# Attention 0 of a two-layer encoder: three kinds of small transfers issued from GpSimd's queue instead of SyncE's

## The chip, the cores and the metric

The kernel runs on one NeuronCore of a Trainium2 chip. The core has five engines with a queue of instructions each: TensorE (PE, with its weight loads shown as PEld), VectorE (DVE), ScalarE (ACT), GpSimd (POOL) and SyncE (SP), which here does nothing but issue DMAs. Engines wait for each other and for DMAs through semaphores, and a waiting instruction holds all that stands behind it in its queue. The metric is device time in microseconds of one execution, lower is better; times compared are medians of several runs.

## The reference

Two layers work on 1024 tokens of width 1024 in f32. Layer 0, which the change is about, is differential attention with 8 heads. Each head has two query/key pairs of width 64 (c = 0, 1) and values of width 128:

```
sc = einsum('bqhcd,bkhcd->bhcqk', qb, k) * scale
p  = softmax(sc); p = p[:, :, 0] - lam * p[:, :, 1]
o  = einsum('bhqk,bkhd->bqhd', p, v)
o  = rmsnorm(o, subln_g) * (1 - lambda_init)
y  = (o.reshape(b, s, 1024) * silu(z)) @ w_out
```

q, k, v and z are one projection of the normalised input; q and k are turned by a rotary embedding. Layer 1 is latent attention with 8 heads, whose queries have a part without and a part with rotary embedding. Each layer ends in an output projection, a gate and a residual, and a last norm closes the trunk.

## The kernel before, in words

Every f32 operand of a matmul is split into a high part (a cast to fp32r) and a low part (the difference), and a product is three matmuls: high by high, low by high, high by low. In layer 0 the queries of a head have only 64 rows for each c, so high and low keys are stacked in one tile of 128 rows, and the query parts are stored twice. `stack_q` (L361 to L370) makes these tiles for one head and one half of the tokens (512): ScalarE casts the high part `qa` (L364, L365), GpSimd subtracts the low part `qb` (L366, L367), each into one group of 64 partitions, and four DMAs of 128 KB copy them to the other 64 partitions (L369, L370, for `qa` and then for `qb`). The scores (L866) of c = 0 need the first copy of each, those of c = 1 the second. Layer 1 uses the same helper for its rotary query parts (tiles `qpa`, `qpb`).

Attention 0 is a loop over 8 heads of 8 tiles of 128 queries. A tile (`q_tile`) computes scores, two softmaxes and their difference; between its pieces TensorE takes steps of `stream0`, the projections of the next head's k, q and z strips, which are what `rope` and `stack_q` then work on. So a head's query tiles come into being while the head before is computed. `rope` copies the projection to SBUF on ScalarE (L331, L333), swaps rows with four DMAs (L335), and multiplies and adds on GpSimd (L336, L341, L343); the strips' own splits are ScalarE's casts and GpSimd's subtractions (L218, L219).

The tail of a tile (transposes L395, their evictions L397 on ScalarE and L398 on VectorE, the product with v) runs one or two tiles later, in `after_scores`. After a half of a head the output `o` is evicted (L931, L932), multiplied by the gate on GpSimd (L938), and the sum of squares gives the norm: VectorE's few small steps, GpSimd's power (L169) and a small multiplication (L953) yield the factors `y`, 128x4. `finish` applies them. The factors must lie along the free dimension of all partitions, so `bcast_rows` writes them to DRAM (L420, 2 KB) and loads them back spread over all partitions (L422, 256 KB, tile `bc_s`); GpSimd multiplies (L908, `scale`) and a DMA stores the result (L912, `store`, 256 KB). The last half of head 7 goes another way, without these transfers.

The list `hooks` spaces these steps out: what is in it when `after_scores` begins is run at that tile's end, and what a hook appends comes a tile later. Before the change `bcast_rows` is called with the norm, `scale` one tile later (two for the last two halves that take this way), `store` two tiles after `scale`.

A planner orders each engine's instructions from its own estimates. Instructions wrapped in `in_turn` keep the program's order on their engine; nearly all GpSimd work of the attention stages is wrapped. DMAs of SP mostly are not, so the planner may issue them earlier or later than they are written. During attention 0 GpSimd also prepares combinations of the output weights (L1112 to L1123) and of finished outputs (L1145 to L1149), and near its end the splits of the output projection's operands (L1199). SP issues everything: the strips' weights (L197), the rope swaps, the copies, the factors, the stores, the output weights.

Of the kernel before, what the change touches and what calls it, by code (L numbers as in the profile page):

```python
# [11 lines left out]
F32 = mybir.dt.float32  # L12
# [9 lines left out]
P = 128  # L22
# [4 lines left out]
HF = 512  # L27
NH = 8
# [48 lines left out]
def f32v(ap):  # L77
    return ap.bitcast(F32)
# [3 lines left out]
def trunk(ctx: ExitStack, tc: tile.TileContext, A, out):  # L82
    nc = tc.nc
    SP, PE, V, S, G = nc.sync, nc.tensor, nc.vector, nc.scalar, nc.gpsimd

    def pool(stack, name, bufs=1, side="left", space=None):
        kw = dict(name=name, bufs=bufs, reuse_waits="tile")
        if space is not None:
            kw["space"] = space
            if space == DRAM:  # L90
                kw.pop("reuse_waits")
        else:
            kw["side"] = side
        return stack.enter_context(tc.tile_pool(**kw))
# [21 lines left out]
    def bank(tag, name, shape=None):  # L116
        nonlocal turn
        if tag == "acc":
            turn += 1
            if (turn - 1) % (2 + NB.get("accx", 0)) < 2:  # L120
                return psa.tile([P, HF], F32, name=name, tag="acc", bufs=2)
            tag = "accx"
        return ps.tile(shape or [P, HF], F32, name=name, tag=tag, bufs=NB[tag])

    dr = pool(ctx, "dr", bufs=1, space=DRAM)
# [6 lines left out]
    oF = [dr.tile([NH, 2, P, HF], F32, name=f"oF{l}") for l in range(2)]  # L132
# [47 lines left out]
    def behind(eng):  # L180

        return tc.issue_after(mk[eng]) if eng in mk else nullcontext()

    def in_turn(ins):

        return tc.keep_in_program_order(ins) if mk else ins
# [174 lines left out]
    def stack_q(qa, qb, r):  # L361

        with behind("S"):
            S.copy(qa[0:64, 0, :], r[0:64])  # L364
            S.copy(qa[64:128, 1, :], r[64:128])  # L365
        in_turn(G.tensor_sub(qb[0:64, 0, :], r[0:64], f32v(qa[0:64, 0, :])))  # L366
        in_turn(G.tensor_sub(qb[64:128, 1, :], r[64:128], f32v(qa[64:128, 1, :])))  # L367
        for t in (qa, qb):
            SP.dma_start(f32v(t[64:128, 0, :]), f32v(t[0:64, 0, :]))  # L369
            SP.dma_start(f32v(t[0:64, 1, :]), f32v(t[64:128, 1, :]))  # L370

    def store_v(l, sp, acc, tt, fh, tag="vst", bufs=None):
        v = sp.tile([P, 2, HF], F32R, name="v_hl", tag=tag, bufs=bufs or VB[l])
# [43 lines left out]
    def bcast_rows(sp, y, tag, bufs):  # L417

        d_ = dr.tile([HF], F32, name="bc_d", tag="bcd", bufs=4)
        SP.dma_start(d_.rearrange("(p t) -> p t", p=P), y)  # L420
        b = sp.tile([P, HF], F32, name="bc_s", tag=tag, bufs=bufs)
        SP.dma_start(b, d_[None, :].to_broadcast([P, HF]))  # L422
        return b, b.rearrange("p (q t) -> p t q", t=4)

    def t3(ap_):
        return ap_.rearrange("p (t q) -> p t q", t=4)
# [173 lines left out]
    for f in range(2):  # L600
        fs = slice(f * HF, f * HF + HF)
        spread = PE.matmul(cb[:, fs], ones[0:1, :], crow[0:1, fs], start=True, stop=True).ins
# [179 lines left out]
    def q_done(h):  # L782
        def f(acc, half):
            rot, fin = rope(wp, acc, half, SC0, *[G if h else V] * 2)

            def g():
                qa = a0a.tile([P, 2, HF], F32R, name="qa", tag="qs", bufs=4)
                qb = a0a.tile([P, 2, HF], F32R, name="qb", tag="qs", bufs=4)
                stack_q(qa, qb, r.pop() if r else fin())
                QS.setdefault(h, [None, None])[half] = qa, qb  # L790

            r = []
            sum_ = [lambda: r.append(fin()), None] if 0 < h < 5 else []
            side.add(*[None] * ROT, rot, *[None] * (DEF - 1 - ROT - (h == NH - 1)), *sum_, g)
        return f
# [105 lines left out]

    def finish(o, y, l, h, half, dst, ap_, dgs):

        if dst is None:
            b, rb = bcast_rows(ap_, y, "osq", 4)

            def scale():
                in_turn(G.tensor_mul(t3(o), t3(o), rb))  # L908
                hooks.append(lambda: hooks.append(store))

            def store():
                SP.dma_start(oF[l][h, half], o)  # L912

            if l == 0 and (h, half) >= (NH - 2, 1):
                hooks.append(lambda: hooks.append(scale))
            else:
                hooks.append(scale)
            return
        rb = bank("z", "rb") if l else Y[1]
        for j in range(4):  # L920
            js = slice(j * P, (j + 1) * P)
            S.mul(dgs[:, js], ident, y[:, j : j + 1])
            PE.matmul(rb[:, js], ones, dgs[:, js], start=True, stop=True)
        V.tensor_mul(o, o, rb)
# [9 lines left out]
    def subln(o, sq, zz, half, h, dst):  # L934


        if dst is None:
            in_turn(G.tensor_mul(o, o, GZ[h][half]))  # L938
        else:
            V.tensor_mul(o, o, GZ[h][half])  # L940

        def rest():
            pt = Y[0] if dst is not None else ssq_at[0] if ssq_at else bank("acc", "ssq")
            for j in range(4):
                PE.matmul(pt[:, j : j + 1], sq[:, j * P : (j + 1) * P], ones[:, 0:1], start=True, stop=True)
            w = sm.tile([P, 4], F32, name="sl_w")
            fin = sm.tile([P, 4], F32, name="sl_f")
            V.tensor_mul(fin, zz, zz)
            V.scalar_tensor_tensor(out=w, in0=fin, scalar=P * EPS / GUARD ** 2, in1=pt[:, 0:4], op0=ALU.mult, op1=ALU.add)
            V.scalar_tensor_tensor(out=fin, in0=fin, scalar=FMAX / GUARD ** 2, in1=w, op0=ALU.mult, op1=ALU.is_ge)  # L950
            V.tensor_scalar(w, w, 3.0e38, None, op0=ALU.min)
            y = rsqrt(w, 4)
            in_turn(G.tensor_mul(y, y, fin))  # L953
            if dst is not None:
                return lambda: finish(o, y, 0, h, half, dst, None, sq)
            finish(o, y, 0, h, half, None, a0b, sq)

        if dst is None:
            (hooks if h < NH - 1 else rests).append(rest)
        else:  # L960
            return rest()
# [29 lines left out]
    tails, hooks = [None, None], []  # L991
# [171 lines left out]
    class Seven:  # L1163
# [32 lines left out]
        def put(self, raw, hi, lo, eng):  # L1196
            with behind("S"):
                S.copy(hi, raw)  # L1198
            sub = eng.tensor_sub(lo, raw, f32v(hi))  # L1199
            if eng is G:  # L1200
                in_turn(sub)
                self.sub = sub.ins
# [818 lines left out]
    def qp_done(h):  # L2021
        def f(acc, half):
            rot, fin = rope(wp, acc, half, SC1, G, G if h or half else V)

            def g():
                qa = ap.tile([P, 2, HF], F32R, name="qpa", tag="qps", bufs=4)
                qb = ap.tile([P, 2, HF], F32R, name="qpb", tag="qps", bufs=4)
                stack_q(qa, qb, fin())
                QP.setdefault(h, [None, None])[half] = qa, qb

            side.add(None, rot, *[None] * (h > 0 and not half))
            if h and half:
                late_q.append(g)
            elif half:
                first_q.append(g)
            else:
                side.add(g)
        return f
# [35 lines left out]
    def attn1(h, fills, extra=None, late=None):  # L2074
# [5 lines left out]
        def close(half, o_, zz):  # L2080
            if late and half == 1:
                ctx_["late"] = late(o_, zz, ctx_["gz"])
                return
            o = ap2.tile([P, HF], F32, name="o1", tag="o", bufs=2)
            V.scalar_tensor_tensor(out=o, in0=o_, scalar=0.5, in1=ctx_["gz"], op0=ALU.mult, op1=ALU.mult)
            V.reciprocal(zz, zz)
            finish(o, zz, 1, h, half, None, ap2, None)
# [365 lines left out]
```

## Time and profile before

| | us |
|---|---|
| median of 3 runs | 1396.26 (1395.49 to 1396.42) |
| the profiled execution | 1394.95 |
| its span, first to last instruction | 1393.2 |
| TensorE busy | 1367.5 |
| VectorE busy | 928.3 |
| GpSimd busy | 753.1 |
| ScalarE busy | 740.9 |

The granted TensorE clock is 0.999 of full speed. All 230.74 MB of the program's own DMA traffic runs on SP's queue, 52.7% of the time of the 16 DMA engines. Attention 0 lies between 137 us (its first scores) and about 690 us.

How to read it: a row of a group gives line, engine, operation, the tiles written and read, the count, then the busy time and the mean of one, and after the second bar the idle time of the engine before them and what ended it. A row of waits gives total, times and the longest. A row of the timeline gives start and length in us and, in brackets, the idle time before it. SP's issues are sequencer work (SPq) and not counted as busy. TensorE's matmuls overlap and their ends are modelled, so small gaps do not show.

### The profile page before, as it was taken

How to read it: one execution, taken by the hardware profiler on the slowest of the kernel's cores; microseconds unless marked ns; L12 is line 12 of the kernel's file. 1: busy time of each engine (PE TensorE's matmuls, PEld its weight loads, DVE VectorE, ACT ScalarE, POOL GpSimd, SP SyncE). 2: the span in 40 equal slices, each digit the busy share in tenths (PEclk: the TensorE clock that was granted, in tenths of full speed). 3: DMA queues.
4: the chain of work that ended last, by engine and by line, in shares of the span. 5: the costliest groups of instructions: out<-in, count | busy, mean ns of one | idle time of the engine just before them, and what ended most of it. 6: DMA issues, size and time to landing. Idle time of an engine off the chain costs nothing.

```text
span 1393.2 us, 20695 instructions
## 1 busy us (share of the span) xinstructions
PE 1367.5 (98%) x7334; PEld 1144.7 (82%) x7334; DVE 928.3 (67%) x1313; ACT 740.9 (53%) x1339; POOL 753.1 (54%) x593
## 2 busy tenths in 40 slices
PE   9999999999999999999999999999999999999997
PEld 6788888888888887887887888888888888888886
DVE  7655777777666666668596976545656555555684
ACT  5532465656565555567648553335454544545554
POOL 5424374758686858575794233532141373834673
PEclk9999999999999999999999999999999999999999
DMA  9857644343444434526564246489443364667463
GB/s 342 263 177 244 201 110 141 100 144 105 149 127 144 128 121 122 151 61 212 182 219 167 68 137 212 137 282 286 125 105 119 102 201 136 193 221 215 145 245 121
DMA packets 149386, 232.06 MB, mean 167 GB/s; under 512 B 20641, under 2 KB 57633, under 8 KB 149282
## 3 DMA queue, kind: packets, MB, share of 16 engines
q1 hardware_dynamic: 149282, 230.74, 52.7%
q8 instruction: 58, 0.95, 0.3%
q14 instruction: 46, 0.38, 0.1%
HBM read 144.74 MB, written 61.81 MB: 148 GB/s over the span
## 4 chain that ended last, share of the span: by engine, by line
PE 79%; DVE 6%; DMA 5%; ACT 3%; POOL 3%; issue 2%; SPq 1%; POOLq 0%; ACTq 0%; DVEq 0%
PE s L2067 10%; PE acc L173 9%; PE acc L175 9%; PE acc L174 9%; PE tr L395 7%; PE s L866 7%; PE pv L173 4%; PE pv L174 4%; PE pv L175 4%; PE vps L173 2%; PE vps L174 1%; PE vps L175 1%; PE zacc L175 1%; PE zacc L173 1%; PE zacc L174 1%
## 5 line engine op out<-in xcount | busy, mean ns | idle before, releaser
L397 ACT CAST pth<-tr 128x512 fp32r<-128x512 f32 x256 | 150.3, 587 | 285.7 <-PE tr L395 280.8
L412 DVE TENSOR_REDUCE nm<-s 128x1 f32<-128x1024 f32 x192 | 233.8, 1218 | 79.8 <-PE s L866 70.9
L398 DVE TENSOR_TENSOR ptl<-tr,pth 128x512 fp32r<-128x512 f32 x256 | 176.1, 688 | 150.3 <-ACT pth L397 146.3
L219 POOL TENSOR_TENSOR wl<-wraw,wh 128x512 fp32r<-128x512 f32 (+2 forms) x77 | 98.8, 1284 | 208.4 <-ACT wh L218 176.3
L414 ACT ACTIVATE e<-s,nm 128x1024 f32<-128x1024 f32 x128 | 143.5, 1121 | 35.4 <-DVE nm L412 35.0
L395 PE MATMUL tr<-ident,e 128*128 128x128 f32 x1024 | 155.0, 273 | 4.1 <-DVE ptl L398 3.8
L395 PEld LDWEIGHTS tr<-ident,e 128*128 128x128 f32 x1024 | 120.7, 140 | 46.5 <-DVE ptl L398 24.1
L173 PE MATMUL acc<-h0h,wh 128*128 128x512 f32 x360 | 150.2, 417 | 0.0
L173 PE MATMUL pv<-pth,vt 128*128 128x256 f32 x512 | 147.5, 288 | 0.0
L174 PE MATMUL pv<-ptl,vt 128*128 128x256 f32 x512 | 145.6, 284 | 0.0
L175 PE MATMUL pv<-pth,vt 128*128 128x256 f32 x512 | 144.6, 282 | 0.0
L175 PE MATMUL acc<-h0h,wl 128*128 128x512 f32 x360 | 141.5, 393 | 0.0
L174 PE MATMUL acc<-h0l,wh 128*128 128x512 f32 x360 | 141.1, 392 | 0.0
L336 POOL TENSOR_TENSOR rp_r<-rp_raw,cosT 128x512 f32<-128x512 f32 x36 | 47.0, 1305 | 104.4 <-ACT rp_raw L333 52.9
L173 PEld LDWEIGHTS pv<-pth,vt 128*128 128x128 f32 x512 | 97.2, 190 | 2.9 <-ACT pth L397 0.2
L174 PEld LDWEIGHTS pv<-ptl,vt 128*128 128x128 f32 x512 | 97.4, 190 | 2.4
L175 PEld LDWEIGHTS pv<-pth,vt 128*128 128x128 f32 x512 | 97.3, 190 | 0.0
L1199 POOL TENSOR_TENSOR wol<-wol,woh 128x512 fp32r<-128x512 f32 x56 | 82.3, 1492 | 26.0 <-ACT woh L1198 24.4
L866 PE MATMUL s<-ks,qa 128*128 128x512 f32 x256 | 82.7, 403 | 4.4 <-DVE e L874 3.2
L874 DVE SCALAR_TENSOR_TENSOR e<-s,z,e 128x1024 f32<-128x1024 f32 x64 | 82.2, 1284 | 2.2
L866 PE MATMUL s<-ks,qb 128*128 128x512 f32 x256 | 79.8, 393 | 1.2 <-DMA qb<-qb 1.2
L175 PEld LDWEIGHTS acc<-h0h,wl 128*128 128x128 f32 x360 | 67.6, 188 | 15.1
(427 smaller groups left out, 3461.1 us busy)
## 6 DMA issues: line engine op xcount, KB each, us to landing
ada<-in_ada_ss SPq DMA_DIRECT2D x32, 512.0 KB, 5.9
wraw<-in_w_s SPq DMA_DIRECT2D x64, 256.0 KB, 2.8
vS<-v_hl SPq DMA_DIRECT2D x32, 512.0 KB, 5.9
vt<-vS SPq DMA_DIRECT2D x32, 512.0 KB, 4.9
wol<-tS SPq DMA_DIRECT2D x56, 256.0 KB, 5.2
tS<-ob SPq DMA_DIRECT2D x48, 256.0 KB, 2.0
rp_sw<-rp_raw SPq DMA_DIRECT2D x160, 64.0 KB, 2.0
bc_s<-bc_d SPq DMA_DIRECT2D x34, 256.0 KB, 4.2
```

The costliest lines, as they stand in the source:

```text
L173: PE.matmul(psum, ah, bh, start=first, stop=False, skip_group_check=skip)
L174: PE.matmul(psum, ah, bl, start=False, stop=False, skip_group_check=skip)
L175: mm3.last = PE.matmul(psum, al, bh, start=False, stop=last, skip_group_check=skip).ins
L219: sub = (V if pair_of else G).tensor_sub(l_[:, :n], raw[:, :n], f32v(h_[:, :n]))
L395: transpose_p.last = PE.transpose(tr[:, j, :], p[:, kt * P : (kt + 1) * P], ident).ins
L397: mk["S"] = S.copy(pth[kh][:, :, dst], tr).ins
L398: mk["V"] = V.tensor_sub(ptl[kh][:, :, dst], tr, f32v(pth[kh][:, :, dst])).ins
L412: mk["V"] = V.reduce_max(nm, s_ps, axis=AX.X, negate=True).ins
L414: mk["S"] = S.activation(e, s_ps, AF.Exp, bias=nm, scale=1.0, accum_out=zs).ins
L866: PE.matmul(s_ps[:, kc * HF : (kc + 1) * HF], src[:, c, ql], KS[h][kc][:, c, :], start=fst, stop=not fst)
L1199: sub = eng.tensor_sub(lo, raw, f32v(hi))
L2067: PE.matmul(s_ps[:, kc * HF : (kc + 1) * HF], lhs, rhs(kc), start=i == 0, stop=i == 4)
```

## The change

The copies of `qb` are issued by GpSimd, in its program order, directly after the two subtractions; those of `qa` stay with SP. As the helper is shared, this holds for layer 1's `qpb` too. In layer 0 the write of the norm factors and the store of the scaled output are issued by GpSimd, also in program order: the write directly after the factors' multiplication, the store directly after the scaling instead of two tiles later. The load of the spread factors stays with SP but becomes a hook of its own, one tile after the write, with the scaling one more tile later for every half. For the last two halves, which took the longer way before, the scaling stays where it was.

```diff
-        for t in (qa, qb):
-            SP.dma_start(f32v(t[64:128, 0, :]), f32v(t[0:64, 0, :]))
-            SP.dma_start(f32v(t[0:64, 1, :]), f32v(t[64:128, 1, :]))
+        for t, put in (qa, SP.dma_start), (qb, lambda *a: in_turn(G.dma_start(*a))):
+            put(f32v(t[64:128, 0, :]), f32v(t[0:64, 0, :]))
+            put(f32v(t[0:64, 1, :]), f32v(t[64:128, 1, :]))
...
     def finish(o, y, l, h, half, dst, ap_, dgs):
 
+        if dst is None and l == 0:
+            d_ = dr.tile([HF], F32, name="bc_d", tag="bcd", bufs=4)
+            in_turn(G.dma_start(d_.rearrange("(p t) -> p t", p=P), y))
+
+            def spread():
+                b = ap_.tile([P, HF], F32, name="bc_s", tag="osq", bufs=4)
+                SP.dma_start(b, d_[None, :].to_broadcast([P, HF]))
+
+                def scale():
+                    in_turn(G.tensor_mul(t3(o), t3(o), b.rearrange("p (q t) -> p t q", t=4)))
+                    in_turn(G.dma_start(oF[l][h, half], o))
+
+                hooks.append(scale)
+
+            hooks.append(spread)
+            return
         if dst is None:
             b, rb = bcast_rows(ap_, y, "osq", 4)
...
-            if l == 0 and (h, half) >= (NH - 2, 1):
-                hooks.append(lambda: hooks.append(scale))
-            else:
-                hooks.append(scale)
+            hooks.append(scale)
             return
```

## The prediction

> **What bounds the kernel now.** I read the page's busy shares first, then the busy time of each engine in attention 0 (first scores at 137 us, last tile at 690), then who waits for whom there, then the timelines around the query copies. TensorE carries the time:
>
> ```profile
> PE 1367.5 (98%) x7334; PEld 1144.7 (82%) x7334; DVE 928.3 (67%) x1313; ACT 740.9 (53%) x1339; POOL 753.1 (54%) x593
> ```
> ```profile
> 137.00:690.00 553.00, 543.56 (x3033) 458.45 (x3032) 394.00 (x560) 324.92 (x575) 371.02 (x301) 1.00 0.45 136
> 395.00:470.00 75.00, 73.54 (x411) 62.00 (x410) 49.84 (x71) 43.83 (x78) 59.77 (x50) 1.00 0.43 131
> ```
>
> The columns of the windows are length, then busy PE, PEld, DVE, ACT, POOL. In the 553 us that the change mainly touches, TensorE is idle 553 - 543.6 = 9.4 us: that about caps any gain, and every microsecond by which TensorE is made to wait there comes out at the end, since it is as full after as before. GpSimd (POOL) is 67% busy over the stage, but 59.8 of 75 us, 80%, in the stretch where it also prepares the output weights.
>
> What TensorE waits for there (total, times, longest):
>
> ```profile
> PE s L866 <- DVE e L874: 3.2, 6, 1.0
> PE tr L395 <- DVE ptl L398: 2.8, 5, 0.9
> PE s L866 <- DMA qb<-qb: 1.2, 2, 0.7
> PE s L866 <- DMA qa<-qa: 0.9, 1, 0.9
> ```
>
> Only the last two rows, 2.1 us, are transfers of the kind that the change moves. SP's queue, from which everything leaves now, does stand still:
>
> ```profile
> SPq L912 <- POOL o L908: 57.5, 14, 6.7
> SPq L197 <- POOL wl L219: 48.0, 29, 4.6
> SPq L420 <- POOL rq_y L953: 41.8, 12, 9.9
> ```
>
> The store of the scaled outputs (L912) and the write of the norm factors (L420) hold SP for 99 us in all, and both go away. But SP idle is only worth what TensorE waited for behind it: the 2.1 us, and what comes through ScalarE, whose copy of the high query part waits for GpSimd's rope sum and stands ahead of its evictions:
>
> ```profile
> ACT qa L364 <- POOL rp_r L343: 9.5, 6, 2.3
> ```
>
> **The change part by part.** GpSimd gets 78 issues: 32 copies of low query parts in layer 0 and 16 in layer 1 (the same helper serves both), 15 writes of norm factors, 15 stores of outputs (all heads and halves but the last). SP loses the same 78.
>
> *What one issue costs GpSimd.* No DMA leaves GpSimd's queue in this trace. From SP the copies cost and land like this (ns minimum, median, maximum; landing in us):
>
> ```profile
> L367 POOL TENSOR_TENSOR qb<-rp_r,qa x16: 1276/1292/2185, 118.8 to 627.7; 64x512 fp32r<-64x512 f32 x16
> L369 SPq DMA_DIRECT2D qb<-qb x16: 461/468/752, 123.1 to 628.8; - x16
> L370 SPq DMA_DIRECT2D qb<-qb x16: 461/462/736, 123.9 to 629.4; - x16
> ```
> ```profile
> DMA to landing us min/median/max: 2.2/2.3/5.7
> ```
>
> One bound is SP's 0.46 us for the same copy; the other is GpSimd's own pass over the same 64 rows, 1.29 us. A gain from the issue itself is excluded: GpSimd does nothing of the kind today. I take 1.0 us, an estimate nearer to GpSimd's row, because the same engine would do it. The Trainium skill (DMA: Bandwidth & Descriptors, section "Latency and other measured facts") puts the first byte at about 1 us from GpSimd's queue against about 0.6 from SP's; read as the hold of the queue it gives the same sum as my 1.0, and no row here shows it. The same page, under "Issuing engines are not separate DMA queues", says that issuing from more engines saves only the issuing sequencer's time; by that rule what SP gains here is the waits above and no bandwidth.
>
> Of landing I take the 2.3 us less the 0.46 of issue, 1.8 us after the issue is done.
>
> *The low query copies.* Before, SP issues the first as soon as the first subtraction is done, while GpSimd runs the second. Now both issues are queued on GpSimd behind both subtractions, so the first scores of a half head can start g + 1.8 us after the second subtraction, with g the issue: 2.8 us at 1.0. What there is, from the issue of the second copy (which SP makes at once when the second subtraction ends) to TensorE's first use, for heads 3, 5, 6 and 7:
>
> ```profile
> L370 SPq DMA_DIRECT2D qb<-qb x1: 461/461/461, 338.2 to 338.2; - x1
> L866 PE MATMUL s<-ks,qb x1: 389/389/389, 341.4 to 341.4; 128*128 128x512 f32 x1
> ```
> ```profile
> L370 SPq DMA_DIRECT2D qb<-qb x1: 461/461/461, 477.0 to 477.0; - x1
> L866 PE MATMUL s<-ks,qb x1: 387/387/387, 480.3 to 480.3; 128*128 128x512 f32 x1
> ```
> ```profile
> L370 SPq DMA_DIRECT2D qb<-qb x1: 467/467/467, 547.2 to 547.2; - x1
> L866 PE MATMUL s<-ks,qb x1: 468/468/468, 551.3 to 551.3; 128*128 128x512 f32 x1
> ```
> ```profile
> L370 SPq DMA_DIRECT2D qb<-qb x1: 461/461/461, 617.6 to 617.6; - x1
> L866 PE MATMUL s<-ks,qb x1: 389/389/389, 620.4 to 620.4; 128*128 128x512 f32 x1
> ```
>
> Head 4's stand in the timelines (start, length, and for TensorE the wait before it):
>
> ```profile
> 407.14 1.29 POOL L367 TENSOR_TENSOR qb<-rp_r,qa 64x512 fp32r<-64x512 f32 x1
> ```
> ```profile
> 411.22 0.70 PE L866 MATMUL s<-ks,qb 128*128 128x512 f32 x2 [0.55 <-DMA qb<-qb]
> ```
>
> So there are 3.2, 2.8, 3.3, 4.1 and 2.8 us for heads 3 to 7, against the 2.8 needed: spare 0.4, 0, 0.5, 1.3, 0. The cover is all but used up, and whatever makes the subtractions themselves later goes through to TensorE. The second halves are first used four tiles (553 / 64 = 8.6 us each) after the first ones, far more than is needed, and cost nothing.
>
> *What makes the subtractions later.* In program order the norm factors' write stands right behind L953, just ahead of the subtractions in heads 3, 5, 6 and 7: 1.0 each. The store stands behind the scaling (L908), and the scaling moves one tile, 8.6 us, later:
>
> ```profile
> L908 POOL TENSOR_TENSOR o<-o,bc_s 128x512 f32<-128x512 f32 x15 | 23.2, 1549 | 16.9 <-DMA bc_s<-bc_d 16.8
> ```
>
> In the dense stretches GpSimd has little idle time to absorb them. The last wait before the subtractions of heads 3, 4, 5 and 7:
>
> ```profile
> 324.01 1.29 POOL L938 TENSOR_TENSOR o<-o,gz 128x512 f32<-128x512 f32 x1 [0.39 <-ACT o L932]
> ```
> ```profile
> 386.35 1.29 POOL L341 TENSOR_TENSOR rp_sw<-rp_sw,sinT 128x512 f32<-128x512 f32 x1 [1.95 <-DMA rp_sw<-rp_raw]
> ```
> ```profile
> 454.95 1.29 POOL L341 TENSOR_TENSOR rp_sw<-rp_sw,sinT 128x512 f32<-128x512 f32 x1 [0.43 <-DMA rp_sw<-rp_raw]
> ```
> ```profile
> 603.24 1.28 POOL L938 TENSOR_TENSOR o<-o,gz 128x512 f32<-128x512 f32 x1 [4.07 <-ACT o L932]
> ```
>
> Head 7 thus starts afresh 11 us before its subtractions. Lateness of the subtractions: head 3, a write and a store less 0.4, 1.6, and up to 1.5 more if the moved scaling (1.55 us) falls into the full stretch: taken 2.0. Head 4, a store and the scaling, 2.55, less the 1.95 us wait: 0.6. Head 5, two writes and a store less 0.4: 2.6. Head 6, a write and a store: 2.0. Head 7, a write: 1.0. Less the spare: 1.6 + 0.6 + 2.1 + 0.7 + 1.0 = 6.0 us of new TensorE waits. In heads 5 and 6 part of this shows not at the scores but at ScalarE's copy (L364), which then waits longer for L343 with the evictions queued behind it; it is the same delay, counted once. Head 2 has 273.1 - 266.5 = 6.6 us (the row's first scores are still head 1's) and costs nothing:
>
> ```profile
> L866 PE MATMUL s<-ks,qb x3: 389/389/397, 267.0 to 273.1; 128*128 128x512 f32 x3
> L370 SPq DMA_DIRECT2D qb<-qb x1: 461/461/461, 266.5 to 266.5; - x1
> ```
>
> If that cover went, it would be another 1 or 2 us; head 1, whose GpSimd work is as sparse, I put with it.
>
> *Layer 1's copies.* GpSimd is lightly loaded there. The first pair alone is tight, with 2.3 us for 2.8:
>
> ```profile
> L370 SPq DMA_DIRECT2D qpb<-qpb x1: 461/461/461, 943.0 to 943.0; - x1
> L2067 PE MATMUL s<-kps,qpb x1: 389/389/389, 945.3 to 945.3; 128*128 128x512 f32 x1
> ```
>
> That is 0.5 us. The later pairs are made a head ahead of their use by the program's order, and I count nothing for them; without that cover it would be up to 0.5 us each.
>
> *Spread factors one tile later, store on GpSimd.* SP's load of them no longer waits for the write to land, and GpSimd no longer waits for the load. These waits of GpSimd shrink:
>
> ```profile
> POOL rp_sw L341 <- DMA rp_sw<-rp_raw: 18.1, 9, 4.3
> POOL o L908 <- DMA bc_s<-bc_d: 16.8, 5, 5.7
> ```
>
> Most of it lies where GpSimd has time. The first kind comes right after the query subtractions, where SP's rope swaps wait behind the query copies:
>
> ```profile
> 477.04 0.46 SPq L370 DMA_DIRECT2D qb<-qb  x1
> 477.60 2.45 SPq L335 DMA_DIRECT2D rp_sw<-rp_raw  x4
> ```
> ```profile
> 481.69 1.29 POOL L341 TENSOR_TENSOR rp_sw<-rp_sw,sinT 128x512 f32<-128x512 f32 x1 [3.30 <-DMA rp_sw<-rp_raw]
> ```
>
> The swaps can now leave some 2 us sooner, but GpSimd spends two issues there in their place, 2.0 of the 3.3 us. I count 0.5 us back in the whole stage. The output buffers come free earlier; nobody waits for them.
>
> *Sum.* 6.0 + 0.5 - 0.5 = +6.0 us. The profiled execution took 1394.95 us, 1393.2 of it span, so it becomes 1401; the median of the runs shown, 1396.26, becomes **1402.3**. With the issue at 0.46 the need is 2.3 us, nearly all is absorbed, and the sum is +0.5; at 1.29 it is 3.1 us and the five heads give 2.6, 1.2, 3.2, 1.6, 1.6, with 0.8 for layer 1: +10.5.
>
> **The rivals.** *The issue is cheap and lost in the cover.* It decides at about 0.5 us an issue, SP's price: +0.5, 1397. For it speaks that SP's row is the only one of a DMA issue; against it, that the only rows of GpSimd's own over these 64 partitions cost 1.29.
>
> *Faster: the copies get out from behind SP's queue.* Head 6's copy took 4.90 us instead of 2.3, behind loads that SP had issued before it:
>
> ```profile
> 546.28 4.90 DMA qb<-qb
> ```
>
> If a queue of its own lets it land in 2.3, the swaps leave sooner and the issue costs under 0.3 us, then the 2.1 us of DMA waits go, and about 2 of the 9.5 us that ScalarE waits for GpSimd: -4, 1392. Against it: one copy in five is late, and the move itself puts the first copy behind the second subtraction. The same DMA page, in "Queues, rings and completion order", lets each DMA engine take turns between the queues' rows, which is what this case needs; no run here has two queues of data.
>
> *Slower still: issues that stretch.* One of the subtractions took 2185 ns against 1292, so GpSimd's work can be held up by others. If a 128-row issue costs as much as the scaling (1.55 us) and a 64-row one 1.29, the dense stretch, 80% full, runs over, and two or three more heads lose 2 us each: +15, 1411. The Trainium skill (SBUF — State Buffer, "Who interferes with whom") has GpSimd and VectorE block each other on a shared port for some pairs of instructions, descriptor writing included.
>
> *The change does less than it says*, if the planner leaves SP's loads of the factors where they were: SP then still waits for the write to land, and the sum keeps its 6.0 without the 0.5.
>
> **How the numbers follow.** My own sum 0.48, with a range of its own from 1398.5 to 1408; the cheap issue 0.23; faster 0.17; stretched issues 0.12. The range of 1392 to 1412 takes in all four ends. A measurement of this kernel can tell about 0.2%, 2.8 us, from no change: slower 0.60, the same 0.23, faster 0.17.
>
> **What would show it.** In the changed profile: DMA rows on POOL, 78 of them, near 1.0 us each, and POOL near 430 us busy in attention 0 instead of 371; the L912 and L420 waits of SP gone in layer 0; waits of TensorE for the qb copies at the first tile of heads 3 to 7 up from 1.2 to some 5 us; ScalarE's wait at L364 longer. The prediction is wrong if the issues come out under 0.5 us, or if the copies land in time although they cost 1 us, which would mean that GpSimd's idle time lies closer to the subtractions than I read it.

## The result, and the profile after

The changed kernel takes 1415.6 us (median of 4 runs, 1414.15 to 1417.16) against 1396.34: a ratio of 1.0139, interval [1.0122, 1.0157], 19 us slower. The forecast was 1402.3 with a range up to 1412: right in sign, a third of the size. In the profiled execution (1415.74, span 1414.0) the page has TensorE and the new queue at:

```profile
PE 1371.2 (97%) x7334; PEld 1148.0 (81%) x7334; DVE 937.6 (66%) x1313; ACT 741.2 (52%) x1339; POOL 796.3 (56%) x671
q0 software_dynamic: 3984, 10.26, 2.5%
```

GpSimd's 78 issues are there. The groups by line and shape show the price of one (busy, mean ns, then the idle time just ahead and what ended it):

```profile
L368 POOL DMA_DIRECT2D qb<-qb x32 | 17.3, 546 | 0.0
L906 POOL DMA_DIRECT2D bc_d<-rq_y x15 | 9.3, 622 | 5.6 <-POOL rq_y L966 3.9 <-PE tr L395 0.9 <-PE s L866 0.8
L914 POOL DMA_DIRECT2D oF<-o x15 | 8.8, 589 | 5.9 <-POOL o L913 5.5 <-DMA qa<-qa 0.4
```

A copy holds GpSimd 0.55 us. A factor write or a store holds it 0.6 us and stands some 0.4 us more ahead of it (3.9 us over 10 times, 5.5 over 14), because it reads what GpSimd itself has just written: 1.0 us in all. Who waits in 137 to 705 us (total, times, longest), TensorE first, then ScalarE, then SP:

```profile
PE tr L395 <- DVE ptl L398: 6.1, 8, 2.3
PE s L866 <- DVE e L874: 6.1, 6, 1.2
PE s L866 <- DMA qb<-qb: 2.6, 3, 1.7
PE oy L174 <- POOL wol L1212: 2.1, 1, 2.1
PE s L866 <- DMA qa<-qa: 1.1, 1, 1.1
PE oy L175 <- POOL oal L1212: 0.9, 1, 0.9
```
```profile
ACT qa L364 <- POOL rp_r L343: 19.1, 6, 7.1
```
```profile
SPq L910 <- DMA bc_d<-rq_y: 51.2, 10, 17.3
```

TensorE waits 18.9 us there instead of 8.8. Only 1.4 of the 10.1 new ones are for a qb copy; 6.2 are for VectorE's parts of the softmax and the transposes. Where that was followed, in head 5 below, they come late because ScalarE's evictions stand behind a cast that waits for GpSimd's rope sum (L364, 19.1 us over the stage instead of 9.5, and 8.1 of the 9.6 new ones in head 5). The store and write waits of SP are gone, and a new one stands in their place: the load of the spread factors (L910) is queued behind a write that GpSimd issues late.

Where the 20 us lie can be read by setting the start of every matmul beside that of the same matmul in the trace of before (medians at the borders of the stretches; before's time, us). The first stretch has no changed work: what it shows, 0.2 to 3.3 us in the kernels below, is from run to run. The columns are the kernels of the experiments; *held* is to be read against *later*, its kernel without the holds.

| stretch | after | copies only | finish only | later | held | copies, att. 0 | held copies | evict first |
|---|---|---|---|---|---|---|---|---|
| 0-137 | 1.4 | 0.9 | 0.6 | 2.1 | 1.5 | 0.2 | 0.6 | 1.3 |
| 137-332 | 0.7 | 0.3 | 0.9 | -0.1 | 0.6 | 0.3 | 0.3 | 0.1 |
| 332-400 | 1.0 | 0.0 | -0.3 | 0.0 | 0.5 | 0.0 | 0.1 | 0.0 |
| 400-465 | 1.7 | 0.5 | 1.6 | -1.5 | 0.1 | 0.9 | 0.5 | 1.8 |
| 465-540 | 5.1 | 2.6 | 3.7 | 2.0 | 3.2 | 2.4 | 0.1 | -0.4 |
| 540-608 | -0.5 | -0.5 | 1.4 | -1.3 | 1.1 | -0.4 | -0.6 | -0.6 |
| 608-712 | 4.9 | 0.8 | 6.7 | 2.4 | 8.0 | 0.7 | 0.0 | 1.2 |
| 712-930 | 0.5 | -0.5 | -0.6 | -0.5 | -0.4 | 0.9 | 0.4 | 0.3 |
| 930-1100 | 5.8 | 5.3 | 0.9 | 0.1 | 0.4 | 0.1 | -0.1 | 0.2 |

Three places carry it: head 5 (465-540), the end of attention 0 (608-712) and layer 1's first pair (930-1100).

**Head 5.** GpSimd's timeline in after (start, length, then the idle time ahead):

```profile
478.04 1.28 POOL L343 TENSOR_TENSOR rp_r<-rp_r,rp_sw 128x512 f32<-128x512 f32 x1
479.27 1.04 POOL L169 TENSOR_TENSOR rq_y<-sl_w,mhalf 128x4 f32<-128x4 f32 x1
480.39 0.20 POOL L966 TENSOR_TENSOR rq_y<-rq_y,sl_f 128x4 f32<-128x4 f32 x1
481.00 0.62 POOL L906 DMA_DIRECT2D bc_d<-rq_y  x1 [0.41 <-POOL rq_y L966]
...
485.47 1.06 POOL L368 DMA_DIRECT2D qb<-qb  x2
486.60 1.28 POOL L336 TENSOR_TENSOR rp_r<-rp_raw,cosT 128x512 f32<-128x512 f32 x1
489.26 1.29 POOL L341 TENSOR_TENSOR rp_sw<-rp_sw,sinT 128x512 f32<-128x512 f32 x1 [1.38 <-DMA rp_sw<-rp_raw]
490.63 1.29 POOL L343 TENSOR_TENSOR rp_r<-rp_r,rp_sw 128x512 f32<-128x512 f32 x1
```

ScalarE there, and what TensorE makes of it:

```profile
479.35 0.62 ACT L364 CAST qa<-rp_r 64x512 fp32r<-64x512 f32 x1 [4.90 <-POOL rp_r L343]
...
491.95 0.62 ACT L364 CAST qa<-rp_r 64x512 fp32r<-64x512 f32 x1 [7.08 <-POOL rp_r L343]
492.60 0.62 ACT L365 CAST qa<-rp_r 64x512 fp32r<-64x512 f32 x1
493.24 0.59 ACT L397 CAST pth<-tr 128x512 fp32r<-128x512 f32 x1
```
```profile
482.49 0.66 PE L395 MATMUL tr<-ident,e 128*128 128x128 f32 x4 [2.28 <-DVE ptl L398]
```

ScalarE stands 4.90 and 7.08 us for the two rope sums; an eviction (L397) comes out behind each pair of casts. In before it waited 3.9 us for the same two sums, and at the second place the eviction stood ahead of the casts:

```profile
482.10 0.59 ACT L397 CAST pth<-tr 128x512 fp32r<-128x512 f32 x1 [4.61 <-PE tr L395]
484.38 0.62 ACT L364 CAST qa<-rp_r 64x512 fp32r<-64x512 f32 x1 [1.70 <-POOL rp_r L343]
```

**The end.** GpSimd in after, in the scaling of the last factors:

```profile
687.87 1.57 POOL L913 TENSOR_TENSOR o<-o,bc_s 128x512 f32<-128x512 f32 x1 [2.27 <-DMA bc_s<-bc_d]
689.85 0.58 POOL L914 DMA_DIRECT2D oF<-o  x1 [0.41 <-POOL o L913]
690.45 1.28 POOL L1212 TENSOR_TENSOR oal<-oal,oah 128x512 fp32r<-128x512 f32 x1
691.68 2.51 POOL L1212 TENSOR_TENSOR wol<-wol,woh 128x512 fp32r<-128x512 f32 x2
```
```profile
693.00 0.50 PE L174 MATMUL oy<-wol,oah 128*128 128x512 f32 x1 [2.07 <-POOL wol L1212]
```

The wait of 2.27 us for the factors, 0.41 us ahead of the store and its 0.58 us, 3.3 us together, stand ahead of the splitting of the output weights that TensorE then waits for. In before none of the three was there (the scaling at 674.75 had no wait, the next split followed at 676.26). For these last half heads the scaling has kept its place; it is the load of the factors that the change puts one tile later.

**Layer 1's first pair.** SP and GpSimd in after, then SP in before:

```profile
956.64 1.41 SPq L377 DMA_DIRECT2D vS<-v_hl  x2
958.14 1.27 SPq L197 DMA_DIRECT2D wraw<-in_w_qn  x1
959.51 2.85 SPq L386 DMA_DIRECT2D vt<-vS  x2
```
```profile
957.64 1.13 POOL L368 DMA_DIRECT2D qpb<-qpb  x2
```
```profile
941.76 0.55 SPq L369 DMA_DIRECT2D qpb<-qpb  x1
942.97 0.46 SPq L370 DMA_DIRECT2D qpb<-qpb  x1
943.54 1.68 SPq L377 DMA_DIRECT2D vS<-v_hl  x2
```

Before, the two stores of 512 KB were queued behind the copies, and a copy landed 2.6 us after its issue. After, SP has nothing to hold them back and issues the stores first; the copies share the DMA engines with them and land 6.4 us after their issue. TensorE waits 3.94 us, and is slow behind it:

```profile
964.13 0.72 PE L2080 MATMUL s<-kps,qpb 128*128 128x512 f32 x2 [3.94 <-DMA qpb<-qpb]
964.67 0.61 PE L173 MATMUL vps<-wvh,ckh 128*128 128x512 f32 x1
965.08 0.63 PE L174 MATMUL vps<-wvl,ckh 128*128 128x512 f32 x1
...
968.32 0.39 PE L173 MATMUL vps<-wvh,ckh 128*128 128x512 f32 x1
968.54 0.40 PE L174 MATMUL vps<-wvl,ckh 128*128 128x512 f32 x1
```

From 964.67 on eight matmuls start 0.43 us apart, from 968.32 on 0.23: 1.6 us more are lost when the wait is over. Together that is 5.5 of the 5.8 us. For some 40 us from here the planner also orders TensorE and ScalarE otherwise than before; little of the loss is left for that.

### The profile page after: what moved, and what is told of

Read it like the earlier page. It is cut to its first block, busy times and chain, and to the rows that moved or that the text cites. A ratio compares the mean times of both kernels' runs of the same rounds, so it can differ in the third digit from the quotient of the medians.

```text
span 1414.0 us, 20712 instructions
## 1 busy us (share of the span) xinstructions
PE 1371.2 (97%) x7334; PEld 1148.0 (81%) x7334; DVE 937.6 (66%) x1313; ACT 741.2 (52%) x1339; POOL 796.3 (56%) x671
## 4 chain that ended last, share of the span: by engine, by line
PE 82%; DVE 5%; DMA 4%; POOL 3%; ACT 3%; issue 2%; SPq 0%; POOLq 0%; ACTq 0%; DVEq 0%
PE s L2080 10%; PE acc L173 9%; PE acc L175 9%; PE acc L174 9%; PE tr L395 7%; PE s L866 7%; PE pv L173 4%; PE pv L174 4%; PE pv L175 4%; PE vps L173 1%; PE vps L174 1%; PE vps L175 1%; PE oy L175 1%; PE oy L174 1%; PE oy L173 1%
## 5 line engine op out<-in xcount | busy, mean ns | idle before, releaser
L397 ACT CAST pth<-tr 128x512 fp32r<-128x512 f32 x256 | 150.2, 587 | 285.2 <-PE tr L395 283.8
L174 PE MATMUL pv<-ptl,vt 128*128 128x256 f32 x512 | 145.8, 285 | 0.0
L174 PE MATMUL acc<-h0l,wh 128*128 128x512 f32 x360 | 141.6, 393 | 0.0
L174 PEld LDWEIGHTS pv<-ptl,vt 128*128 128x128 f32 x512 | 97.9, 191 | 2.5
```

The costliest lines, as they stand in the source:

```text
L174: PE.matmul(psum, ah, bl, start=False, stop=False, skip_group_check=skip)
L397: mk["S"] = S.copy(pth[kh][:, :, dst], tr).ins
```

## The experiments

Times are medians of a chip's runs; before, run beside them, took 1395.7 to 1397.3, and the ratios are to it. Theory A: what costs is GpSimd's time. Theory B: transfers land later from its queue. Theory C: SP is held behind transfers that GpSimd issues late.

**The change in two halves.** *Copies only*: before with the change's loop in stack_q. *Finish only*: the changed kernel with before's loop there.

> Only the low copies go to GpSimd's queue, in both layers; the finish is as before. Theory A (GpSimd's time: each issue holds GpSimd some 0.55 us, so that the rope's sums, and with them ScalarE's queue, come later): the copies are 32 of the 64 issues in attention 0 and bring no waits of their own, so they carry a third of the 10 us that heads 2 to 7 lost, 3 to 4 us, and all of the 6 us in layer 1: 1405 to 1407 us. Theory B (a copy issued from GpSimd lands later, 3.2 us after its issue against 2.3): they carry nearly all of the heads' loss too: 1411 to 1413 us.

> Only the finish changes: norm factors and scaled outputs from GpSimd's queue, spread factors one tile later; all copies as before on SyncE. Theory A: GpSimd is held 16 times for about 0.6 + 0.6 us and waits some 0.9 us for its own results, the larger part of what was added, so heads 2 to 7 lose 6 to 7 us and the tail 2 us: 1404 to 1405 us. Theory B: nothing in the heads waits for these transfers, so only the tail's 2 us are left: 1398 to 1399 us.

Copies 1405.5, ratio 1.0064 [1.0044, 1.0083]; finish 1409.8, 1.0098 [1.0082, 1.0114]. The parts, 9 and 14 us, make up the whole 19 and a little more. The finish alone, with which no score waits for a moved transfer, speaks against B as the whole cause, and cost half as much again as A had for it. The copies lost 5.3 us in layer 1, and before it little but head 5.

**Layer 1's copies back on SP, and the finish without GpSimd.**

```
stack_q(qa, qb, r, low=None):  ... (qa, SP.dma_start), (qb, low or SP.dma_start)   # low: GpSimd, in layer 0
```

> The whole change in attention 0, but layer 1's low copies stay on SyncE. Both theories: the 4.9 us at layer 1's first pair and the 1.0 us at its second head go, and TensorE's order there is again that of before: 1409 to 1410 us. If layer 1's loss came from attention 0's delay (it did not start from the copies), the time stays at 1415.

The second has the changed finish with both G.dma_start as SP.dma_start, and before's copies:

> Only the place of the finish changes: spread one tile later, scale one tile after it and its store at once, all DMAs on SyncE, no issue from GpSimd. Theory A: GpSimd does what it did before, so the heads lose nothing; the tail, whose scaled outputs come later, loses up to 2 us: 1396 to 1398 us. A third theory (the later finish itself delays what the heads and the tail need): 1400 us or more.

1411.9, 1.0104 [1.0089, 1.0119], and 1398.0, 1.0005 [0.9996, 1.0015]. Layer 1's loss is its own and comes from the queue of its copies: its stretch falls from 5.8 to 0.5 us. One tile later by itself is no measurable loss, though the end of attention 0 shows 2.4 us in this profile too.

**Time without transfers.** The finish of the last kernel, with two extra subtractions of 128x384 in GpSimd's order where the issues stood:

```
+    def hold(d):
+        in_turn(G.tensor_sub(d[:, 0:384], d[:, 0:384], d[:, 0:384]))
...
             SP.dma_start(d_.rearrange("(p t) -> p t", p=P), y)
+            hold(dgs)
...
                     SP.dma_start(oF[l][h, half], o)
+                    hold(b)
```

> The finish one tile later with its DMAs on SyncE (that kernel took 1398), plus two extra GpSimd subtractions of 128x384 on data that is dead by then, one where the factors' issue stood in GpSimd's order and one where the store's stood. Such a subtraction took 1.0 us (1015 ns in the trace of after), an issue 0.6 us with 0.4 us of waiting ahead of it. Nothing is issued from GpSimd. Theory A (GpSimd's time is what costs): the 12 us of the finish alone come back, 1408 to 1411 us. Theory C (SyncE is held behind transfers that GpSimd issues late: it waited up to 17 us for the factors to land before it could load them): without those transfers 1398 to 1401 us.

1411.7, 1.0122 [1.0104, 1.0141]: as much as the finish itself, or a little more, with no DMA on GpSimd, and each hold took 0.83 us, not the 1.0 of the expectation. TensorE, ScalarE and VectorE run in the same order here as in the kernel without the holds, so no other order of these engines is at work. For the finish, A stands: GpSimd's time at these two points is enough to make the loss. Against *later* in the table, 5.6 us of it lie at the end of attention 0 and the rest in the heads.

**Which issue, and SP's wait.** *Spread later*: finish only, with hooks.append(lambda: hooks.append(spread)). *Store* and *factor*: only one of the two transfers on GpSimd.

> The finish alone on GpSimd's queue (1409.8 us), with the load of the spread factors and all behind it yet one tile later, so that SyncE comes to it when the factors have landed. Theory A: GpSimd is held as before, 1407 to 1411 us. Theory C: SyncE's 47 us of waits at that load shrink to a few and most of the 12 us with them, 1398 to 1402 us.

> The finish one tile later, with only the store of the scaled outputs on GpSimd's queue (one issue a half head, about 1 us of GpSimd with the wait ahead of it); the factors' write on SyncE. Theory A: about half of the 12 us, 1402 to 1405 us, or less if the loss grows faster than the time added. Theory C: nobody waits for this store in the heads, 1398 to 1400 us.

> The finish one tile later, with only the factors' write on GpSimd's queue; the store on SyncE. Theory A: about half of the 12 us, 1402 to 1405 us. Theory C: the long waits of SyncE for these factors are all here, 1408 to 1410 us.

1426.9, 1.0225 [1.0210, 1.0241]; 1407.9, 1.0088 [1.0073, 1.0104]; 1405.4, 1.0071 [1.0056, 1.0086]. C falls: SP's wait at that load went from 46.8 to 25.6 us and the kernel lost 17 us more. The store alone costs nearly as much as both, the factor alone two thirds: the losses share their waits and don't add. And the same GpSimd work one tile later costs more than twice as much, so its amount alone does not settle the price. Why this place is so much dearer was not taken apart. The trace shows two things that come on top: TensorE waits 3.15 us (at 270.06) behind a VectorE instruction that was held beside GpSimd (last section), and it runs at half clock for 27 us of attention 0 instead of 10.

**GpSimd relieved.** The gate multiplication (128x512, 1.29 us a half head) off GpSimd, in the changed kernel and in before:

```
-            head_out(o_, o, sq)
+            S.activation(sq, o_, AF.Square, scale=1.0 / GUARD)
+            V.scalar_tensor_tensor(out=o, in0=o_, scalar=g8[:, 0:1], in1=GZ[h][half], op0=ALU.mult, op1=ALU.mult)
...
-            in_turn(G.tensor_mul(o, o, GZ[h][half]))
```

> The changed kernel, with the gate multiplication of a half head (128x512, 1.29 us on GpSimd, 15 in attention 0) taken off GpSimd: VectorE forms the gated output from PSUM in one instruction, and ScalarE's scaling of it (0.69 us) goes too. If the loss in attention 0 is GpSimd's time ahead of the rope's sums, about 1.3 of the 3 us added to a half head come back and some 5 to 9 of the 13 us with them: 1406 to 1411 us (layer 1's 6 us stay). If it is not GpSimd's time: 1414 to 1417 us.

> The kernel before with the same edit and nothing else. If GpSimd's time is what the heads wait for already there (TensorE waits 8.8 us in attention 0), a few of these go: 1391 to 1395 us. If that time is covered, or VectorE is late in its place: 1396 to 1399 us.

1410.3, 1.0100 [1.0082, 1.0117]; 1394.5, 0.9987 [0.9978, 0.9996]. From 137 to 608 us the loss of the changed kernel falls from 7.9 to 4.7 us. But from the same edit before gains 3.0 us there, so that between the two relieved kernels the change still costs 7.7: less work on GpSimd helps both, and the pair does not show that it makes the change cheaper. The edit also takes ScalarE's scaling of the output away, so it is not GpSimd's time alone. The end stays (5.9), and layer 1's 5.8 became 2.7, with a wait for its first copies of 1.9 us instead of 3.9 and the clock whole behind it (1.00 from 959 to 965); this edit touches nothing there, and why the wait is shorter is not explained. The second kernel is 1.8 us faster than before, 0.13%.

**Another queue for layer 1's copies.** Before, with those copies from ScalarE's queue (S.dma_start).

> The kernel before, with only layer 1's low copies taken off SyncE's queue, issued from ScalarE's instead of GpSimd's. TensorE's order in layer 1 becomes that of the changed kernel. In the changed kernel such copies landed 6.4 us after their issue and TensorE waited 3.9 us for the first pair; from SyncE they took 2.4 us. If it is GpSimd's queue that lands late: about 2.4 us again, and the first pair waits under 1 us, in all 1396 to 1400 us. If the DMA engines were busy with the stores that SyncE now issues ahead of the copies: 5 to 6 us again, a wait of 3 to 4 us, and 1401 to 1405 us.

1417.9, 1.0149 [1.0133, 1.0165], a miss in the time: ScalarE now issues copies that wait for GpSimd's subtractions (up to 7.3 us, ahead of its next eviction), and layer 1's later heads lose 16 us. TensorE waits only 1.1 us for the first pair, not 3 to 4. But the landing of the copies of the first two heads, the point of the run, is:

```profile
DMA to landing us min/median/max: 4.5/4.6/6.4
```

The 6.4 is the first pair's, as from GpSimd's queue. So it is not GpSimd's queue that lands late: off SP's queue, the copies lose their place ahead of SP's stores, which SP issued right behind its own two copies here too.

**Attention 0's copies.** *Copies, att. 0*: before with only these on GpSimd. *Held copies*: before with every transfer in its place and one extra subtraction behind each query stack:

```
+            in_turn(G.tensor_sub(r[:, 0:384], r[:, 0:384], r[:, 0:384]))
```

> The kernel before, with only attention 0's low copies on GpSimd's queue (32 issues of 0.55 us; finish and layer 1 as before). In the run with both layers' copies there attention 0 lost 3 us, so 1398 to 1400 us. If the loss of attention 0 came with layer 1's planned order instead: 1395 to 1397 us.

> The kernel before, with every transfer where it was and the order of the other four engines unchanged, and one extra GpSimd subtraction of 128x384 (1.0 us, on rope data that is dead by then) behind the two subtractions of each of attention 0's 16 query stacks: the time that the two issues took, without the transfers. If GpSimd's time makes the copies' loss in attention 0: 1398 to 1400 us, like the run beside it. If it is the copies' landing (3.2 us against 2.3): 1395 to 1397 us.

1400.8, 1.0032 [1.0020, 1.0045]; 1396.6, 1.0005 [0.9996, 1.0014]. Here A falls: behind the subtractions 0.83 us of GpSimd (the two issues took 1.1) cost nothing that can be measured. A third cause showed in ScalarE's timeline of the first:

```profile
485.90 0.62 ACT L364 CAST qa<-rp_r 64x512 fp32r<-64x512 f32 x1 [6.96 <-POOL rp_r L343]
486.55 0.62 ACT L365 CAST qa<-rp_r 64x512 fp32r<-64x512 f32 x1
487.19 0.59 ACT L397 CAST pth<-tr 128x512 fp32r<-128x512 f32 x1
```

With the copies moved, the planner put these two casts ahead of an eviction that preceded them before (482.10 above). That swap is the only difference in ScalarE's order; TensorE's is unchanged, and VectorE's has one change just behind it (L802).

**The eviction first again.** The stacking of that query half emitted behind the next transposes, in the kernel with attention 0's copies and in the changed one (the casts then come one exponential later than in before):

```
+                put = lambda: stack_q(...)
+                later.append(put) if (h, half) == (5, 1) else put()
...
         mk["V"] = V.tensor_sub(ptl[kh][:, :, dst], tr, f32v(pth[kh][:, :, dst])).ins
+        while later:
+            later.pop()()
```

> The kernel with only attention 0's low copies on GpSimd's queue (1400.8 us), with the stacking of one query half (head 5, its second half) put into the program behind the next transposes, so that ScalarE evicts those transposes ahead of the two casts, as it did in the kernel before; TensorE's and SyncE's orders stay as they are. If the copies' loss in attention 0 is that order of ScalarE (it waited 7.0 us for the rope's sum with the eviction behind it): 2 to 3 us back, 1397 to 1399 us. If it is the copies' landing: 1400 to 1402 us.

> The changed kernel with the same move of that one stacking. If the order of ScalarE there makes part of head 5's 5 us: 1411 to 1413 us. If not: 1414 to 1417 us.

1398.5, 1.0009 [0.9999, 1.0019]; 1414.9, 1.0128 [1.0110, 1.0145]. With the eviction ahead again, and VectorE's L802 back in its place, most of what attention 0's copies cost is gone: head 5 went from 2.4 us to -0.4. In the changed kernel head 5 gave back 1.9 us (5.1 to 3.2), but the end lost more (9.4 instead of 4.9), so nothing that can be measured came of it. In that profile TensorE's clock stood at half twice in the stretch of the end, in the one of after not at all (last section).

**The last finishes on SP.** The changed kernel, with SP.dma_start for (h, half) >= (NH - 2, 1).

> The changed kernel, with the finishes of the last two half heads that have one issued from SyncE (still one tile later). In the changed kernel the end of attention 0 lost 3 to 4 us, with TensorE 2.1 us behind GpSimd's splitting of the output weights. If the last issues on GpSimd held that splitting: 2 to 4 us back, 1411 to 1413 us. If that splitting is late from what the earlier heads left behind: no change, 1414 to 1416 us.

1414.8, 1.0139 [1.0123, 1.0154], no change: the issues of these two half heads do not make the end's loss. TensorE's wait for the weights' splitting is still 1.4 us (2.1 in after), and GpSimd still waits 2.2 us for its factors ahead of it.

## Why the prediction was wrong

*The issue price* (1.0 us, by GpSimd's own row over 64 partitions): 0.55 us for a copy, so near the lower bound; 1.0 us for a factor write or a store, but made of 0.6 us and a wait for GpSimd's own result, which the sum did not have. GpSimd was busy 393.6 us in 137 to 690, not 430. (At 0.46 us the forecast's own terms give -0.5, not its +0.5: every lateness is then within the spare.) The Trainium skill's 1 us against 0.6 (DMA: Bandwidth & Descriptors) is not the hold measured here.

*The low copies in heads 3 to 7*: the step "the first scores of a half head can start g + 1.8 us after the second subtraction" mattered little. TensorE's waits for qb came to 2.6 us, not 5, and an equal hold in their place cost nothing. What attention 0's copies did cost, 4.5 us, came mostly by a road that was not in the text: the planner's order in head 5, of ScalarE above all.

*What makes the subtractions later* is the step that failed most. The lateness was there, but it was charged only to the scores' wait for the copies, less a spare; the road through ScalarE's cast (L364) was "counted once" as the same delay. It is the larger one in the heads, because evictions are queued behind that cast, and no spare at the scores covers it: head 5 lost 5.1 us, with ScalarE's waits for the two sums up from 3.9 to 12.0 us, while TensorE's waits for qb rose by 1.4 in the whole stage. Shown: the finish alone, with no low copy moved, costs 14 us, and two holds without transfers, which leave the order of TensorE, ScalarE and VectorE as it was, cost as much.

*"GpSimd no longer waits for the load"* of the factors: it does, 8.0 us in two places instead of 16.8 in five, and one of the two is new: 2.27 us at the end, ahead of the weights' splitting. The sum had nothing for this stretch, which lost 4.9 us. In every kernel with the load one tile later TensorE waits for that splitting (L174 on `wol`, 0.9 to 4.0 us), in before not at all; *later* loses 2.4 us there without any issue or hold. Why the other kernels lost 3.2 to 9.4 is settled in part: the granted clock goes with it (last section), and the planner has ScalarE's casts for the splitting and one eviction in another order there than in before, which no run took by itself.

*Layer 1*, 0.5 us: it lost 5.8, 5.5 of them at the first pair, as the text placed it. The failed number is the landing, 2.3 us taken and 6.4 measured, and the half clock behind the wait came on top.

*SP's 0.5 us back*: not to be seen. "SP's load of them no longer waits for the write to land" did not come true; it waits 51.2 us for that, which the last rival had foreseen, though by way of the planner.

*The clock*: no term. Of the 12.8 us lost in 137 to 712, 10.1 are waits; the rest goes with the matmuls that run at half speed for 3.4 us at a time (last section).

Of the rivals, "issues that stretch" came near in size (1411) and is refuted as a mechanism: the longest copy issue took 0.73 us. "The issue is cheap" was right about the price and wrong about the cover. "Faster" had the copies land sooner; their median went from 2.2 us to 2.8. The planner did change things, though not where the text looked for it.

## What to carry to other kernels

An instruction put into a busy engine's order is priced by what is queued behind it, not by its length: two holds of 0.8 us a half head cost 16 us where results come behind them that another in-order engine waits for (the rope's sums, the split weights), and one of them behind the query subtractions nothing. A queue also keeps transfers back: before a small copy is moved to a queue of its own, look at which large ones it was holding up. And where a planner orders the engines, compare the orders first; undoing one swap on ScalarE gave back some 3 us.

## What the runs showed of the hardware

*Behind a wait TensorE can run at half its clock.* The first two windows begin where a wait of 2.28 us (after) and one of 2.27 us (layer 1's copies on SP) end, at the same matmul; the other two lie around after's wait of 3.94 us (the granted clock is the third column from the end):

```profile
482.49:487.99 5.50, 5.50 (x28) 5.13 (x29) 4.03 (x6) 2.14 (x5) 5.25 (x6) 0.69 0.62 169
```
```profile
484.83:490.33 5.50, 5.37 (x36) 4.68 (x36) 4.05 (x6) 2.14 (x5) 5.28 (x6) 1.00 0.65 181
```
```profile
964.00:968.00 4.00, 3.87 (x10) 3.12 (x11) 1.23 (x1) 1.71 (x3) 0.00 (x0) 0.58 1.03 359
968.00:972.00 4.00, 4.00 (x21) 3.25 (x20) 1.88 (x3) 0.68 (x3) 0.00 (x0) 0.99 1.15 345
```

At the lower clock TensorE counts as busy but starts about half as many matmuls (0.43 us apart instead of 0.23). The Trainium skill (TensorE: Matmul & The Clock Gate, "What's actually happening") halves the clock after an idle window of about 3.4 us and restores it after as long a busy one. The rows agree on the half and on the length of the recovery (964.67 to 968.07). The length of the wait did not decide: this wait of head 5 was 2.27 to 2.31 us in seven kernels, all under the page's window, and the clock behind it was 0.69 in five of them and 1.00 in two (layer 1's copies on SP, last on SP).

Nor is the half clock always a loss: those two lost as much in head 5 (4.8 and 5.2 us) as after (5.1), since TensorE waited 1.0 to 1.3 us more there instead. At the end of attention 0 it goes with the loss. Where the clock stayed whole there, the kernels lost 2.4 to 5.5 us (later, factor, last on SP, after, layer 1's copies on SP); with one stretch of 3.4 us at half, 5.9 to 8.0 (after with the gate moved, finish only, held); with 6.8 us at half, 9.2 to 11.9 (store, after with the eviction first, spread later). One stretch is 1.7 us of work, so it is part of the difference. Each kernel has one trace, and the clock differs between its executions (0.990 to 0.996 in the four of after), so these are not differences of the kernels alone.

*A tiny VectorE instruction can be held through several of GpSimd's.* In after:

```profile
445.25 3.91 DVE L961 TENSOR_TENSOR sl_f<-zz 128x4 f32<-128x4 f32 x1
```
```profile
444.09 2.54 POOL L1125 TENSOR_TENSOR ob<-ob,c 128x512 f32<-128x512 f32 x2
446.58 1.30 POOL L219 TENSOR_TENSOR wl<-wraw,wh 128x512 fp32r<-128x512 f32 x1
447.83 1.29 POOL L341 TENSOR_TENSOR rp_sw<-rp_sw,sinT 128x512 f32<-128x512 f32 x1
449.20 1.30 POOL L343 TENSOR_TENSOR rp_r<-rp_r,rp_sw 128x512 f32<-128x512 f32 x1
```

It is 128x4 and took 0.15 us at its fastest; here it ended at 449.16, in the first pause of GpSimd (449.12 to 449.20). In the spread-later kernel a VectorE instruction of usually 1.28 us (L436, at 262.93) took 4.74: GpSimd ran without a pause up to 266.58, and its next subtraction (266.65) then took 2.14 us instead of 1.29. The Trainium skill (SBUF — State Buffer, "SBUF: two separate sides") has the two lock a shared port for the length of an instruction; in these rows the hold outlasts three of GpSimd's. It is not what makes the finish's loss: in the held kernel, which lost as much, this instruction never took more than 1.03 us.

*GpSimd's queue is not slow of itself.* In attention 0 its copies landed in 2.5 us (copies, att. 0) and 2.8 (after), against 2.2 from SP.
